# Operand distances, decays as products of gates, and a late root mean square in a two-block transformer kernel

## The chip, the cores and the metric

The kernel runs on one core of a Trainium2 chip. The metric is the device time of one launch in microseconds; the times below are runs of the same program with the same inputs.

## The reference

256 tokens of width 1024 pass through two kinds of blocks in float32. The first block has two layers of a hybrid mixer and an MLP with squared ReLU; the second has one layer of neighbourhood, dilated and memory attention and a mixture of 32 experts. The change touches the first block's mixers most.

```python
h = rms_norm(x, norm_mix[l])
(sq, sk, sv, dq, dk, dv, iq, ik, iw, hq, hf, hi, hg,
 g_sb, g_dsa, g_hg) = jnp.split(h @ w_in_l, ...)
# hgrn2, per head, chunk by chunk:
f = lb + (1.0 - lb) * sigmoid(hf);  k = 1.0 - f;  q = silu(hq)
b = cumsum(log f);  decay[t, s] = exp(b[t] - b[s]) for s <= t
att = einsum('tk,sk,tsk->ts', q, k, decay);  o = att @ hi + (q * exp(b)) @ S
# mixed = sigmoid(g_sb) * y_sb + sigmoid(g_dsa) * y_dsa + sigmoid(g_hg) * y_hg
x = x + mixed @ w_out_l
x = x + square(relu(rms_norm(x, norm_mlp[l]) @ w_up[l])) @ w_down[l]
```

y_sb comes from stick-breaking attention, y_dsa from a sparse attention that picks its 64 best keys by an index score, y_hg from the recurrence above.

## The kernel before

Each projection is done in three products of float32r parts (`mm3`: high times high, low times high, high times low). A weight tile comes in by a DMA on SP's queue into a ring of four tiles (`load`), ScalarE copies its high part and VectorE subtracts the low one (`split`). `proj_rows` takes tokens as the stationary and weights as the moving operand and gives rows of tokens; `proj_cols` takes weight blocks of 128 columns as the stationary and all 256 tokens as the moving operand and gives columns. The transposed parts of x, `xh` and `xl`, are made by a norm: `norm` squares x on ScalarE, takes the power on POOL, scales the rows on VectorE, transposes them on TensorE and splits them; `late_norm` transposes the unscaled x and leaves the factor to a later place (the MLP takes its square into the last addition). The two mixers use `norm`, the MLPs and the second block `late_norm`.

A mixer's projections are a list of chunks. `stream` prepares the next chunk (load and split) before the present chunk's products. At each yield of a chunk `step` moves the tasks that run beside it: the sparse attention (`dsa`, 1.5 steps a turn), the recurrence (`hgrn`, 3.5 steps, HG_RATE) and the stick-breaking attention (`sb`, 1.5). The order is that of the index and key projections, the recurrence's three, the gate of the recurrence, the stick-breaking projections, the two other gates, then the branches' output products and `w_out`. `dsa` waits with its softmax part until the recurrence's output is there; at the last gate `sigmoids` steps the tasks until all three outputs are there.

The recurrence works on levels of 64, 32, ... 1 tokens. For each level a 0/1 matrix (`lev`) sums the logarithms of the gates between a token and the middle of its block: TensorE multiplies the transposed, split logarithms `gh`, `gl` with it (`decays`, L679 and L680), ScalarE takes the exponential into `z`, VectorE and POOL multiply its halves with keys and queries (`scale`, L693 and L695), TensorE makes the small products (L715), and `join` puts them together.

Tiles lie in SBUF in the order in which the pools are opened: from the left the constants, the small tiles, the ring, `xh` and `xl`, then the tiles of 4 KB (`p4`), of 2 KB and the first block's own; from the right the tiles of 8 KB (`p8`) and the high and low parts of the weights (`split`). The distances between operands follow from the sizes of what lies between.

The experts' weights (192 pieces of 1 MB) are loaded into tiles as the dense stage frees them, and the expert stage runs through them in order.

Of the kernel before, what the change touches and what calls it, by code (L numbers as in the profile page):

```python
# [42 lines left out]
HG_RATE, DS_RATE, SB_RATE, NA_RATE, MEM_RATE, DIL_RATE = 3.5, 1.5, 1.5, 1.25, 1.5, 1.5  # L43
WAIT_X = {"km": 4, "qa0": 4, "qa1": 4, "ka": 5, "qm": 5, "qd": 4, "kd": 4}
WAIT_I, WAIT_O = 4, 7
WAIT_G, WAIT_H, WAIT_P, WAIT_S, WAIT_U = 3, 2, 2, 0, 2
# [4 lines left out]
C_MIX, C_MLP, C_MIX2, C_FFN2, C_MEM, C_LB, C_ON, C_QK, N_COLS = 0, 16, 32, 40, 48, 56, 64, 66, 72  # L51

# [3 lines left out]
def _constants():  # L56
# [8 lines left out]
    mats, sels = [], []  # L65
    for h in LEVELS:
        m = np.zeros((128, 128))
        for p in range(128):
            r = p // (2 * h) * 2 * h + h - 1
            if p > r:  # L70
                m[r + 1:p + 1, p] = 1
            else:
                m[p + 1:r + 1, p] = 1
        mats.append(m)
        if h < 32:

            s, t = i[:, None] % 32, i[None, :32]
            sels.append((s // (2 * h) == t // (2 * h)) & (s % (2 * h) < h) & (t % (2 * h) >= h))
    c["lev"] = np.concatenate(mats + [i[:, None] > i[None, :]] + mats[4:] + [i[:, None] <= i[None, :]], axis=1)
# [16 lines left out]
LATE = ("lev", "sel", "suffix")  # L96
CONST_AT, CONSTS = _constants()
N_KEEP = CONST_AT["lev"][0]
# [4 lines left out]
class Core:  # L103


    def __init__(self, tc, ctx, a, ring=4):
        self.tc, self.nc, self.a, self.ctx = tc, tc.nc, a, ctx
        nc = self.nc
        self.const = ctx.enter_context(tc.tile_pool(name="const", bufs=1))
        self.tiny = ctx.enter_context(tc.tile_pool(name="tiny", bufs=6))  # L110
        self.ring = ctx.enter_context(tc.tile_pool(name="ring", bufs=ring))
# [8 lines left out]
        self.tasks, self.of_table, self.set = [], [], None  # L120

    def open_dense(self, low, high):

        pool = lambda ctx, name, bufs, **side: ctx.enter_context(
            self.tc.tile_pool(name=name, bufs=bufs, reuse_waits="tile", **side))
        self.p8 = pool(self.ctx, "p8", 3, side="right")
        self.split_p = pool(low, "split", 4, side="right")
        self.xt = pool(self.ctx, "xt", 1)
        self.p4 = pool(self.ctx, "p4", 8)
        self.p2 = pool(high, "p2", 10)  # L130
        self.new_pool = pool
# [16 lines left out]
    def load_consts(self):  # L148
        nc = self.nc
        x = self.a["x"].rearrange("(t p) d -> p t d", p=128)  # L150
        for t in range(2):
            nc.sync.dma_start(self.x[:, t], x[:, t])
        nc.sync.dma_start(self.cst[:, :128], self.a["consts"][:, :128])
        nc.sync.dma_start(self.cols, self.a["cols"])
# [50 lines left out]
    def split(self, v):  # L205

        nc, k, n = self.nc, v.shape[1], v.shape[2]
        hi = self.split_p.tile([128, 1024], F32R, tag="hi", name="hi")
        lo = self.split_p.tile([128, 1024], F32R, tag="lo", name="lo")
        hi = hi[:, :k * n].rearrange("p (k n) -> p k n", n=n)  # L210
        lo = lo[:, :k * n].rearrange("p (k n) -> p k n", n=n)
        nc.scalar.activation(hi, v, AF.Copy)  # L212
        nc.vector.tensor_sub(lo, v, hi)  # L213
        return hi, lo

    def split_rows(self, v):
# [4 lines left out]
        for k0, k1 in ((0, cut), (cut, k)):  # L221
            if k1 > k0:
                hi, lo = self.split(v[:, k0:k1])
# [28 lines left out]
    def proj_rows(self, src, n, xs, kt, done, by_tile=False):  # L252
# [7 lines left out]
        def chunk(k0, k1):  # L260
# [5 lines left out]
            for i, (t, r) in enumerate(runs):  # L266
                x = xs(t)
# [12 lines left out]
    def proj_cols(self, src, n, xs, kt, done, early=None):  # L280
# [11 lines left out]
        def chunk(i):  # L292
            blocks = min(per, nb - i)
            v = self.load(src[:, i * 128:(i + blocks) * 128], kt, blocks * 128)
            ws = [self.split(v[:, :, j * 128:(j + m) * 128]) for j in range(0, blocks, m)]
# [41 lines left out]
    def norm(self, gain):  # L337


        nc = self.nc  # L340
        parts, ready = [], set()

        def task(t):
            if not parts:
                parts.extend(self.x_parts())
            xh, xl = parts
            x = self.x[:, t]
            xn = self.t4("xn")
            ms, rs = self.small(1, "ms"), self.small(1, "rs")
            nc.scalar.activation(xn, x, AF.Square, scale=1.0 / 32, accum_out=ms)  # L350
            self.rstd(rs, ms)
            for c in (slice(0, 512), slice(512, 1024)):
                nc.vector.tensor_scalar(xn[:, c], x[:, c], rs, None, op0=ALU.mult)
            yield
            yield
            tok = slice(t * 128, t * 128 + 128)
            for k0 in range(0, 8, 4):
                ps = self.ps().rearrange("p (m t) -> p m t", m=4)
                for m in range(4):
                    nc.tensor.transpose(ps[:, m], xn[:, (k0 + m) * 128:(k0 + m + 1) * 128], self.c("ident"))  # L360
                for m in range(4):
                    k = k0 + m
                    g = self.cols[:, gain + k:gain + k + 1]
                    nc.scalar.activation(xh[k][:, tok], ps[:, m], AF.Identity, scale=g)
                    nc.vector.scalar_tensor_tensor(xl[k][:, tok], ps[:, m], g, xh[k][:, tok], op0=ALU.mult, op1=ALU.subtract)  # L365
            ready.add(t)

        def get(t=None, k=8):
            self.until(lambda: ready >= ({0, 1} if t is None else {t}))
            return parts  # L370

        def start(t):
            g = task(t)
            next(g)
            self.start(g)
# [1643 lines left out]
```

## Time and profile before

| | us |
|---|---|
| median of 3 runs | 1496.46 |
| lowest, highest | 1493.56, 1496.97 |
| the profiled execution | 1495.28 |
| its span on the core | 1493.1 |

The profiled execution's time holds its span and 2.2 us around it. TensorE's granted clock was 0.947 on the mean. In the rows below a matmul's duration overlaps that of the next; how fast a stream of them runs is seen from their starts.

### The profile page before, as it was taken

The numbers are of one execution on the slowest core, as the hardware profiler recorded it, in microseconds if no ns is written. First come the engines' busy times: TensorE is split into PE (matmuls) and PEld (weight loads), VectorE is DVE, ScalarE is ACT, GpSimd is POOL, SyncE is SP. The second block draws the span as 40 slices with busy tenths as digits, with TensorE's granted clock in tenths as the row PEclk, the third lists the DMA queues.
The fourth block names the chain that finished last, engine by engine and source line by source line (L and its number), as shares of the span: only waits on it lengthen the run. The fifth ranks groups of instructions, "written<-read, shape, count | busy, mean of one in ns | idle before, by whom it ended". The sixth has DMA issues, their size and how long they took to land. (4 is left out here: it accounts for less than half of the span.)

```text
span 1493.1 us, 34069 instructions
## 1 busy us (share of the span) xinstructions
PE 1346.4 (90%) x14719; PEld 1182.5 (79%) x14719; DVE 746.3 (50%) x1378; ACT 661.0 (44%) x1182; POOL 153.7 (10%) x203
## 2 busy tenths in 40 slices
PE   7999999999999999999999999998777767766675
PEld 7889999989879889999898888897665655555453
DVE  6885768555565966677565565764111111111012
ACT  6664765544445556665454465863111111111111
POOL 2310011000002210020010025440000000000000
PEclk9999999999999999999999999999999978779777
DMA  9534446655546434366656657589999999999996
GB/s 298 173 108 135 133 149 201 197 182 186 197 121 198 148 95 141 109 227 209 219 180 193 234 187 182 161 330 392 387 415 417 415 417 417 416 417 415 404 418 264
DMA packets 172633, 376.40 MB, mean 252 GB/s; under 512 B 8321, under 2 KB 121137, under 8 KB 152641
## 3 DMA queue, kind: packets, MB, share of 16 engines
q1 hardware_dynamic: 169312, 366.67, 68.4%
q0 software_dynamic: 2880, 6.48, 1.5%
q8 instruction: 116, 1.90, 0.5%
q10 hardware_dynamic: 288, 1.05, 0.2%
q14 instruction: 37, 0.30, 0.1%
HBM read 372.07 MB, written 2.10 MB: 251 GB/s over the span
## 5 line engine op out<-in xcount | busy, mean ns | idle before, releaser
L213 DVE TENSOR_TENSOR lo<-w,hi 128x1024 fp32r<-128x1024 f32 (+3 forms) x334 | 387.6, 1163 | 257.5 <-ACT hi L212 256.3
L212 ACT ACTIVATE hi<-w 128x1024 fp32r<-128x1024 f32 (+3 forms) x334 | 333.4, 1001 | 318.5 <-PE ps L231 162.1
L230 PE MATMUL ps<-xh,hi 128*128 128x256 f32 x1120 | 317.4, 283 | 0.0
L232 PE MATMUL ps<-xh,lo 128*128 128x256 f32 x1120 | 312.4, 279 | 0.0
L231 PE MATMUL ps<-xl,hi 128*128 128x256 f32 x1120 | 312.3, 279 | 0.0
L1828 PE MATMUL hp<-we,xs 128*32 128x128 f32 x4096 | 154.5, 301 | 68.7 <-DMA we<-experts 57.2
L230 PEld LDWEIGHTS ps<-xh,hi 128*128 128x128 f32 x1120 | 210.4, 188 | 5.6 <-issue 3.7
L231 PEld LDWEIGHTS ps<-xl,hi 128*128 128x128 f32 x1120 | 210.4, 188 | 0.8
L232 PEld LDWEIGHTS ps<-xh,lo 128*128 128x128 f32 x1120 | 210.5, 188 | 0.0
L1828 PEld LDWEIGHTS hp<-we,xs 128*32 128x32 f32 x4096 | 122.4, 120 | 99.9 <-DMA we<-experts 67.4
L230 PE MATMUL ps<-hi,xh 128*128 128x256 f32 (+3 forms) x368 | 122.4, 334 | 0.0
L231 PE MATMUL ps<-lo,xh 128*128 128x256 f32 (+3 forms) x368 | 119.1, 325 | 0.8 <-DVE lo L213 0.8
L232 PE MATMUL ps<-hi,xl 128*128 128x256 f32 (+3 forms) x368 | 118.7, 325 | 1.2 <-DVE xl L365 1.2
L496 ACT ACTIVATE g<-hp 128x128 f32<-128x128 f32 x32 | 8.9, 277 | 224.9 <-PE hp L1828 224.9
L1869 PE MATMUL yp<-we,gT 128*32 128x128 f32 x2048 | 91.1, 335 | 18.8 <-ACT gT L1839 12.5
L230 PE MATMUL acc<-hi,hh 128*128 128x512 f32 x256 | 101.3, 396 | 0.0
L232 PE MATMUL acc<-hi,hl 128*128 128x512 f32 x256 | 101.1, 395 | 0.0
L231 PE MATMUL acc<-lo,hh 128*128 128x512 f32 x256 | 101.0, 395 | 0.0
L1869 PEld LDWEIGHTS yp<-we,gT 128*32 128x32 f32 x2048 | 71.0, 135 | 33.3 <-ACT gT L1839 20.9
L1833 DVE TENSOR_TENSOR g<-g,hp 128x128 f32<-128x128 f32 x28 | 8.1, 288 | 153.4 <-ACT g L496 153.4
L230 PEld LDWEIGHTS ps<-hi,xh 128*128 128x128 f32 x368 | 69.9, 191 | 5.3 <-issue 1.5
L232 PEld LDWEIGHTS ps<-hi,xl 128*128 128x128 f32 x368 | 69.6, 190 | 4.5 <-DVE xl L365 1.6
(530 smaller groups left out, 2024.9 us busy)
## 6 DMA issues: line engine op xcount, KB each, us to landing
we<-experts SPq DMA_DIRECT2D x155, 1024.0 KB, 17.5
w<-w_in SPq DMA_DIRECT2D x53, 1024.0 KB, 5.3
we<-experts SPq DMA_DIRECT2D x72, 512.0 KB, 15.5
w<-w_up SPq DMA_DIRECT2D x32, 1024.0 KB, 5.5
w<-w_down SPq DMA_DIRECT2D x32, 1024.0 KB, 4.9
w<-w_out SPq DMA_DIRECT2D x12, 1024.0 KB, 5.9
w<-w_in SPq DMA_DIRECT2D x36, 256.0 KB, 4.0
w<-w_in SPq DMA_DIRECT2D x8, 584.0 KB, 4.4
```

The lines of the kernel that those rows point to most:

```text
L212: nc.scalar.activation(hi, v, AF.Copy)
L213: nc.vector.tensor_sub(lo, v, hi)
L230: mm(out, l[0], r[0], start=first, stop=False)
L231: mm(out, l[0], r[1], start=False, stop=False)
L232: mm(out, l[1], r[0], start=False, stop=last)
L496: ins = self.nc.scalar.activation(out, x, func, **more)
L1828: nc.tensor.matmul(hp[j * 32:j * 32 + 32, wi], xs[:, k0 + kk, es], v[kk][:, j * 128:j * 128 + 128], start=k0 + kk == 0, stop=k0 + kk == 7)
L1833: nc.vector.tensor_mul(g, g, hp[:, 1])
L1869: nc.tensor.matmul(yp[j * 32:j * 32 + 32], gT[:, kk * 32:kk * 32 + 32], v[kk][:, j * 128:j * 128 + 128], start=kk == 0, stop=kk == 3)
```

## The change

- `pad_l`, `pad_r`, `pad_o` and the order of the pools put `xh`, `xl`, the tiles of 4 and 8 KB, the split weights and the branch outputs at one residue modulo 512 bytes, and `split` places its parts `at` a chosen offset: 80 floats for column blocks, 48 for rows under 512 wide, and for wider rows 80 in the first block and 0 in the second.
- `norm` is gone. The mixers use `late_norm`; `factors` makes the row factor `rs` for each token tile, and `by_column` spreads it over the partitions as `row`, by a product of ones with a diagonal. The places that read the mixer's projections multiply by one or the other: on ScalarE as a scale, or on VectorE.
- The recurrence has no logarithms, level matrices and exponentials. `whole` holds products of gates over 2, 4, ... 64 tokens (on POOL), and `grow` multiplies keys and queries in place from level to level, from the smallest upwards, both token tiles at once. HG_RATE is 1.
- `sb_project` waits for `dq` instead of `decays`; its queries and keys, and the gates that are not yet switched, leave PSUM through VectorE instead of ScalarE.
- First loads: identity and columns on ScalarE's queue, `load_later` behind the first chunk, `lev` not loaded, `warm` makes two products of zeros and a table load; the router's weights come in one contiguous transfer. The first layer's MLP ends by column halves like the second's.

```diff
-HG_RATE, DS_RATE, ... = 3.5, 1.5, 1.5, 1.25, 1.5, 1.5
+HG_RATE, DS_RATE, ... = 1, 1.5, 1.5, 1.25, 1.5, 1.5
+PAD_L, PAD_R, PAD_O = 8, 80, 40
+AT_COLS, AT_ROWS, AT_WIDE, PAD_W = 80, 48, (80, 0), 128
...
-    def split(self, v):
+    def split(self, v, at):
-        hi = self.split_p.tile([128, 1024], F32R, tag="hi", name="hi")
+        hi = self.split_p.tile([128, 1024 + PAD_W], F32R, tag="hi", name="hi")
-        hi = hi[:, :k * n].rearrange("p (k n) -> p k n", n=n)
+        hi = hi[:, at:at + k * n].rearrange("p (k n) -> p k n", n=n)
...
-                x = xs(t)
+                x = xs(t, k=r[1])
...
+        def factors(pool):
+            get.rs = [factor(t, pool.tile([128, 1], F32, name=f"rs_m{t}")) for t in range(2)]
+            def by_column():
+                get.row = pool.tile([128, T], F32, name="rs_row")
+                diag = self.t2("diag")[:, :T].rearrange("p (t n) -> p t n", t=2)
+                for t in range(2):
+                    nc.vector.tensor_scalar(diag[:, t], self.c("ident"), get.rs[t], None, op0=ALU.mult)
+                yield
+                ps = self.ps()[:, :T]
+                nc.tensor.matmul(ps, self.c("ones"), diag.rearrange("p t n -> p (t n)"), start=True, stop=True)
+                nc.scalar.activation(get.row, ps, AF.Copy)
...
         def q_done(i, ps):
-            k.sigmoid(s, ps)
-            nc.vector.tensor_mul(tile("hq")[:, i:i + 2], ps, s)
+            nc.vector.tensor_mul(q, ps, row(2))
+            k.sigmoid(s, q)
+            nc.vector.tensor_mul(q, q, s)
...
+        nc.vector.tensor_mul(q, hq, hg)
+        for h in reversed(LEVELS[:-1]):
+            whole[h] = tot[:, at:at + 4 * n].rearrange("p (h n) -> p h n", h=4)
+            u = whole[h // 2].rearrange("p h (n u) -> p h n u", u=2)
+            k.tc.keep_in_program_order(nc.gpsimd.tensor_mul(whole[h], u[:, :, :, 0], u[:, :, :, 1]))
...
+        def grow(h, keys, queries):
+            for x, tok, half in ((hk, keys, 0), (q, queries, 1)):
+                x = x[:, :, tok].rearrange("p h (b u w) -> p h b u w", u=2, w=h)[:, :, :, half]
+                w = whole[h][:, :, tok.start // h:tok.stop // h].rearrange("p h (b u) -> p h b u", u=2)[:, :, :, 1 - half]
+                nc.vector.tensor_mul(x, x, w[:, :, :, None].to_broadcast(list(x.shape)))
...
+        for lev in reversed(range(8)):
+            now = [(t, lev, products(t, lev)) for t in range(2)]
+            if lev == 0:
+                grow(64, slice(0, 128), slice(128, 256))
+            elif lev < 7:
+                grow(LEVELS[lev], slice(0, T), slice(0, T))
+            for j in last:
+                join(*j)
+            last = now
+            yield
...
                 g = gates[b][:, i:i + 2]
+                nc.vector.tensor_mul(g, ps, xs.norm.row[:, None, :].to_broadcast([128, 2, T]))
                 if switched:
-                    k.sigmoid(gates[b][:, i:i + 2], ps)
+                    k.sigmoid(g, g)
-                    nc.scalar.activation(gates[b][:, i:i + 2], ps, AF.Copy)
```

## Rows read from the trace of the kernel before

**Rows 1.** The page: engine shares; DMA busy tenths in 40 slices of the span.
```profile
PE 1346.4 (90%) x14719; PEld 1182.5 (79%) x14719; DVE 746.3 (50%) x1378; ACT 661.0 (44%) x1182; POOL 153.7 (10%) x203
...
DMA  9534446655546434366656657589999999999996
```

**Rows 2.** Busy time by stage: stretch, length, engines, granted clock, DMA share, GB/s.
```profile
60.00:120.00 60.00, 59.31 (x825) 52.99 (x824) 51.63 (x133) 35.18 (x59) 5.87 (x8) 1.00 0.38 115
120.00:210.00 90.00, 90.00 (x756) 85.62 (x756) 54.65 (x102) 59.62 (x115) 1.92 (x2) 1.00 0.40 124
...
290.00:437.00 147.00, 147.00 (x917) 131.26 (x915) 79.66 (x79) 67.60 (x78) 0.26 (x2) 1.00 0.57 182
437.00:449.00 12.00, 8.85 (x47) 7.66 (x46) 8.95 (x22) 7.28 (x19) 2.44 (x3) 0.72 0.21 63
...
870.00:1012.00 142.00, 141.78 (x1014) 125.17 (x1012) 96.41 (x185) 103.31 (x209) 64.90 (x74) 1.00 0.73 218
...
1050.00:1493.00 443.00, 316.34 (x6415) 239.54 (x6415) 63.50 (x182) 54.98 (x167) 0.00 (x0) 0.84 0.99 402
```

**Rows 3.** Timeline of TensorE in five stretches: start, duration, line, names, shape.
```profile
88.81 0.50 PE L680 MATMUL ps<-lev,gl 128*128 128x512 f32 x1 [0.69 <-DVE gl L423]
89.15 0.39 PE L679 MATMUL ps<-lev,gh 128*128 128x512 f32 x1
...
90.31 0.40 PE L680 MATMUL ps<-lev,gl 128*128 128x512 f32 x1
...
271.56 0.28 PE L230 MATMUL ps<-xh,hi 128*128 128x256 f32 x1
...
273.37 0.28 PE L231 MATMUL ps<-xl,hi 128*128 128x256 f32 x1
...
299.50 0.28 PE L231 MATMUL ps<-xl,hi 128*128 128x256 f32 x1
...
301.86 0.28 PE L230 MATMUL ps<-xh,hi 128*128 128x256 f32 x1
...
430.15 0.39 PE L230 MATMUL acc<-hi,hh 128*128 128x512 f32 x1
...
436.92 0.40 PE L232 MATMUL acc<-hi,hl 128*128 128x512 f32 x1
...
878.79 0.39 PE L231 MATMUL ps<-lo,memh 128*128 128x512 f32 x1
...
880.15 0.39 PE L231 MATMUL ps<-lo,memh 128*128 128x512 f32 x1
```

**Rows 4.** Groups of TensorE by line and shape: count, busy us, mean ns.
```profile
L230 PE MATMUL ps<-xh,hi 128*128 128x256 f32 x1120 | 317.4, 283 | 0.0
...
L230 PE MATMUL acc<-hi,hh 128*128 128x512 f32 x256 | 101.3, 396 | 0.0
...
L679 PE MATMUL ps<-lev,gh 128*128 128x512 f32 x32 | 14.6, 455 | 0.0
```

**Rows 5.** Timeline of TensorE where the second layer starts.
```profile
438.20 1.06 PE L360 MATMUL ps<-cst,xn 128*128 128x128 f32 x8 [0.89 <-DVE xn L353]
```

**Rows 6.** Timeline of TensorE at the start.
```profile
10.91 0.46 PE L230 MATMUL ps<-hi,xh 128*128 128x256 f32 x1
12.14 0.39 PE L231 MATMUL ps<-lo,xh 128*128 128x256 f32 x1 [0.77 <-DVE lo L213]
```

**Rows 7.** Groups of VectorE by line and shape, 60 to 240 us.
```profile
L695 DVE TENSOR_TENSOR z<-z,hq 128x256 f32<-128x256 f32 x14 | 7.3, 535 | 1.0 <-ACT z L496 1.0
...
L779 DVE TENSOR_TENSOR o<-o,rs 128x512 f32<-128x512 f32 x1 | 0.7, 693 | 2.1 <-POOL rs L324 2.1
```

**Rows 8.** Timeline of POOL and VectorE from 219.5 us, and VectorE's group.
```profile
220.14 8.40 POOL L1072 TENSOR_TENSOR gate<-gate 128x512 f32<-128x512 f32 x4 [91.10 <-ACT hi L212]
...
220.06 0.96 DVE L213 TENSOR_TENSOR lo<-w,hi 128x768 fp32r<-128x768 f32 x1
...
L213 DVE TENSOR_TENSOR lo<-w,hi 128x768 fp32r<-128x768 f32 x12 | 11.5, 956 | 2.5 <-ACT hi L212 2.2
```

## Prediction before the result

> **What bounds the kernel now.** I read the engine shares of the page first, then the table by stage. TensorE is busy 90% of the span and the DMA line turns from 4 to 7 tenths into a solid 9 over the last third [rows 1]. The stages say why [rows 2]. From 60 to 437 us and from 870 to 1012 us TensorE's busy time equals the stage within 1.2%, with the DMA engines at 0.38 to 0.73. From 1050 us on TensorE has 316 of 443 us and the DMA engines 0.99: that stage waits for expert weights. So up to about 1012 us every microsecond taken out of TensorE's stream counts if VectorE keeps up. The expert loads need tiles that the dense stage frees, so when that stage ends earlier they start earlier, by the same amount.
>
> A busy time of matmuls overlaps, so I read starts instead. The same 128x256 product with the same operands starts every 113 ns in one stretch (271.56 to 273.37, 16 steps) and every 118 ns in another (299.50 to 301.86, 20 steps) [rows 3]. The 128x512 products of the MLP start every 233 ns (430.15 to 436.92, 29 steps), those of the memory projection every 227 ns (878.79 to 880.15, 6 steps) [rows 3]. So there are two levels, 4% and 3% apart, at the full clock.
>
> **The decays (gain).** The level matrices go: 32 pairs of 128x512 matmuls in the two layers [rows 4]. Inside a run they start every 0.232 us (89.15 to 90.31, 5 steps) [rows 3], so 64 cost at least 14.8 us. One that follows a wait or a small product lasts 0.1 us longer, 0.50 for 0.39 [rows 3]; the first ones' mean of 455 ns [rows 4] adds 2 us for 32. With a wait of 0.69 us for an operand in each layer [rows 3] and the 16 transposes of the log gates (about 0.11 us, an estimate from the 118 ns of the larger products) I take 20 us. ScalarE's exponentials and logarithm go too; ScalarE has slack (35 of 60 us) [rows 2].
>
> **The norm at the start of the second layer (gain).** Between 437 and 449 us TensorE issued 47 instructions at a granted clock of 0.72, that is partly at 1.2 GHz [rows 2], because the transposes waited for the scaled rows [rows 5]. 16 transposes at 0.11 and 31 products at 0.118 would need 5.4 of these 12 us. The edit transposes the unscaled rows of the first half while the second half's products still run, and the first chunk asks for k below 4 first: 12 products for each of two token tiles, 2.8 us, cover the last additions, transposes and copies. I take 5.5 of the 6.6 us. The square and the power then hide behind that chunk; without that cover they would cost about 2.5 us.
>
> **The start (gain).** The first product starts at 10.91 us, right after the first weights' copy, and the next waits 0.77 us for the low half of the weights [rows 6], while VectorE and ScalarE still make the parts of x. With x transposed as it lands, its parts are ready before the weights are, so the first product stays near 10.9 but the stutter behind it goes: 2 us, between 0 and 3. Moving two small loads from SP's queue to ScalarE's puts the first weight load about 0.9 us forward, behind 1 MB of x all the same; 0.8 MB of level matrices is no longer fetched there. The two products of zeros run while TensorE is idle: nothing. The loads moved to POOL behind the first chunk, the contiguous router load and the new pool for small tiles: nothing, all are used 10 us or more later.
>
> **The distances (gain, uncertain).** Adding up the tiles in the order in which the pools are opened, stationary minus moving address is now, modulo 512 bytes, 192 for column blocks and 320 for rows and for the MLP's second product. After, it is 320 for both kinds of 256-wide product, 192 for the 512-wide rows of the first block and 0 for those of the second. What before shows: 256 wide at 192, both levels, mostly the high one; 256 wide at 320, both; 512 wide at 320, always the high one; 512 wide at 0, the low one. 512 wide at 192 it doesn't show. If all 3,360 products of column blocks (three lines of 1,120) went from 118 to 113.2 ns and all 768 of the MLP (three of 256) from 233.4 to 226.7 [rows 3, 4], that is 16 + 5 = 21 us. Part already runs low, and both levels occur at one distance, so what ran before a product matters too. I take half, 11 us; below nothing, because a stretch that is low now may turn high, at most about a third of the first sum, -5 us.
>
> The Trainium skill, page "TensorE: Matmul & The Clock Gate", section "Step-by-step: what each phase is for", says that the moving operand and the weight load have read ports of their own, so that loading weights takes nothing from the running matmul. By that rule the distances do nothing and this term is 0, the first rival below. The 512-wide pair of spacings agrees badly with it, the 256-wide pair neither way.
>
> **What is added.** Two ones-products of 128x256 with their copy: 1 us on TensorE in all. On VectorE, in the stretch that had 51.63 busy of 60 us [rows 2]: removed are 24 half-level products (14 at 0.535 us, the others near it), two low halves and two end products at 0.69, together 15 us a layer. Added are 15 products of 128x512 with a broadcast operand (0.693 by the nearest row), 10.4 us, and in that stretch eight products with the factor's row at the same price, 5.5 us [rows 7]. So VectorE has 52.5 us in a stretch that TensorE would now do in 50: 2.5 to 3 us a layer, 6 in all. The strided halves may cost as the strided products do now, 0.535 for 256 elements, so 1.07: then 8.5 us a layer, 17 in all; and 0 if the next stretch takes the backlog. I take 6, since one broadcast row of the same size is the nearer one. POOL's six gate products, 2.1 us and less [rows 8], run beside it.
>
> The Trainium skill, page "SBUF — State Buffer", section "Who interferes with whom", says that VectorE with two operands in SBUF and GpSimd reading SBUF shut each other out for a whole instruction. By it the gate products would hold VectorE up to 4.5 us more a layer, which makes the sum 1475. The trace disagrees on VectorE's side: a low half of 128x768 took 0.96 us beside a POOL product and 0.956 on the mean [rows 8], so the sum leaves it out.
>
> **The slower recurrence.** The task now moves one step a turn instead of 3.5. Counting turns: its output comes at turn 45 instead of 35, the sparse attention that waits for it ends at turn 60 instead of 50, and the last gate block is through at 58. The last two turns then run with no projection beside them: 1 us a layer if later branch products fill in, 3 us if not. I take 2 in all.
>
> **Sum.** -20 - 5.5 - 2 - 11 + 1 + 6 + 2 = -29.5. The profiled execution took 1495.28 us, 1.2 below the median of 1496.46: 1495.3 - 29.5 = 1465.8, so 1466.
>
> **Rivals.**
> - The distances do nothing: 1466 + 11 = 1477. For: both levels at one distance. Against: 512-wide at 0 and at 320.
> - VectorE binds in the recurrence: 17 instead of 6, 1477; with the first rival too, 1488. For: 51.63 of 60. Against: 54.65 of 90 us in the stretch behind it [rows 2], which can take a backlog.
> - All goes right: distances 21, no backlog, no idle turns: 1466 - 10 - 6 - 2 = 1448.
> - VectorE stands still beside POOL's gate products. One of 128x512 takes 2.1 us [rows 8], the halves behind it as much again at most: 4.5 us a layer, 9 in all, 1475. Against: 0.96 beside 0.956 [rows 8].
> - Slower: a serial chain. Each level's products read what the two multiplications behind the last level wrote, in place. If TensorE's order puts them at the head, it waits for two at 1.07 and for one weight split of 1.22 ahead of them: 3.36 us for 7 levels in 2 layers, 47 us. That would stand in place of the 6: 1466 + 41 = 1507. It decides from 2.5 us a level on (35 us in all). Against: one turn brings 24 products, 2.7 us of cover.
> - No change: the expert loads set the end whatever the dense stage does: 1495. For: 0.99 from 1050. Against: 0.73 before 1012.
>
> **Chances.** Forecast (1456 to 1472) 0.36, no effect of the distances 0.25, VectorE with or without it 0.12, all right 0.16, POOL 0.02, chain 0.05, no change 0.04. The range that leaves out 2 in 10 is 1444 to 1484. About 0.3%, 4.5 us, is what a measurement of this kernel can tell from no change. Faster 0.90, same 0.05, slower 0.05.
>
> **What would show it.** No level products; no stretch below the full clock near 430 us, and no wait above 0.5 us there; the column blocks at 113 ns and the MLP's second product at 227 ns; VectorE near 10 tenths in the recurrence, but TensorE without waits for it; the dense stage ending near 982 us and the last stage as long as before. It is wrong if the spacings rise to 120 ns, if TensorE waits for VectorE at each level, or if the expert stage grows by what the dense stage lost.

## The result and the profile after

The changed kernel takes 1476.73 us (median of 4 runs, 1474.38 to 1478.39), the one before 1496.2 in the same comparison: a ratio of 0.9872, 95% interval 0.9854 to 0.989. That is 1.3% faster, inside the predicted range of 1444 to 1484, but outside the forecast's own 1456 to 1472 and 10.7 us above the predicted 1466; it lies at the times of three of the rivals (1475 and 1477), so the time alone does not tell which account is right. The profiled execution took 1474.38 us with a span of 1472.6.

The page after the change, as in [rows 1]: engine shares, and the DMA engines' busy tenths in 40 slices.

```profile
PE 1322.0 (90%) x14647; PEld 1164.7 (79%) x14647; DVE 754.3 (51%) x1369; ACT 628.5 (43%) x1099; POOL 148.7 (10%) x205
...
DMA  8645336655547445266656658599999999999997
```

The stages of the changed kernel, answering to [rows 2]: stretch, length, busy time and instructions of each engine, granted clock, DMA share, GB/s.

```profile
60.00:120.00 60.00, 57.28 (x860) 54.31 (x859) 58.48 (x139) 26.27 (x40) 7.24 (x13) 1.00 0.43 133
120.00:210.00 90.00, 88.88 (x745) 83.43 (x745) 60.23 (x110) 53.94 (x103) 1.92 (x2) 1.00 0.42 130
...
430.00:442.00 12.00, 11.10 (x96) 10.81 (x95) 9.01 (x18) 10.15 (x22) 1.58 (x4) 1.00 0.22 56
853.00:994.00 141.00, 140.82 (x1012) 124.79 (x1010) 94.28 (x184) 102.88 (x209) 65.46 (x74) 1.00 0.73 219
1030.00:1472.00 442.00, 315.82 (x6479) 238.28 (x6467) 63.55 (x182) 55.25 (x168) 0.00 (x0) 0.85 0.99 404
```

TensorE is still the bound of the dense stages and the expert stage is as long as before. Three things differ. At 430 us, where the second layer starts, the clock stays at 1.00 and 96 instructions go through in 12 us, for 47 at 0.72 before. From 60 to 120 us VectorE has 58.48 of 60 us, for 51.63, and TensorE stands idle for 2.7 us, for 0.7. And from 120 to 210 us TensorE, which had no hole there, has 1.1 us of them.

For the account I read, in three traces, when TensorE starts a product that every version has. The third trace is the run with the old distances (first experiment): it has every edit but the distances of the weights' tiles. The indexer parts are the transposes for the index score; branch 2 is the recurrence's output product, the first of the three branches.

```
start, us                            before    after   old distances
first product of the indexer parts    45.81    47.54    47.33
first product of branch 2, layer 1   211.33   205.29   206.41
first down product of MLP 1          279.72   276.46   280.02
last down product of MLP 1           436.92   429.56   437.23
indexer parts, layer 2               477.89   465.28   473.27
branch 2, layer 2                    643.50   623.73   632.25
first down product of MLP 2          711.88   696.54   705.73
last down product of MLP 2           870.44   852.88   864.27
last output product of the dense part 1028.29 1010.37  1022.42
last product of the experts         1488.75  1468.15  1481.98
```

Differences between neighbouring lines of the first and the last column give the terms without the distances. Start: +1.5. From the indexer to branch 2, where the decays are grown: -6.4 and -6.6 in the two layers. From branch 2 to the MLP's down products: +5.2 and +5.1. From MLP 1 to the second layer's indexer: -4.9. The rest of the dense part: within 0.3 of 0. Expert stage: -0.9.

### The profile page after: what moved, and what is told of

Read it like the earlier page. It is cut to its first block, busy times and chain, and to the rows that moved or that the text cites. A ratio compares the mean times of both kernels' runs of the same rounds, so it can differ in the third digit from the quotient of the medians.

```text
span 1472.6 us, 33788 instructions
## 1 busy us (share of the span) xinstructions
PE 1322.0 (90%) x14647; PEld 1164.7 (79%) x14647; DVE 754.3 (51%) x1369; ACT 628.5 (43%) x1099; POOL 148.7 (10%) x205
## 5 line engine op out<-in xcount | busy, mean ns | idle before, releaser
L242 PE MATMUL ps<-xh,hi 128*128 128x256 f32 x1120 | 318.2, 284 | 0.0
L242 PEld LDWEIGHTS ps<-xh,hi 128*128 128x128 f32 x1120 | 211.2, 189 | 7.2 <-issue 4.7
L242 PE MATMUL ps<-hi,xh 128*128 128x256 f32 (+3 forms) x368 | 122.0, 333 | 4.1 <-ACT hi L220 3.2
L242 PE MATMUL acc<-hi,hh 128*128 128x512 f32 x256 | 99.9, 390 | 0.0
L1840 PEld LDWEIGHTS yp<-we,gT 128*32 128x32 f32 x2048 | 66.4, 128 | 41.3 <-ACT gT L1810 21.3
L242 PEld LDWEIGHTS ps<-hi,xh 128*128 128x128 f32 x368 | 70.3, 191 | 8.1 <-ACT hi L220 3.5
L243 PEld LDWEIGHTS ps<-lo,xh 128*128 128x128 f32 x368 | 70.5, 191 | 3.3 <-DVE lo L221 0.8
```

Of the source, the lines that this page charges most:

```text
L242: mm(out, l[0], r[0], start=first, stop=False)
L243: mm(out, l[0], r[1], start=False, stop=False)
L1840: nc.tensor.matmul(yp[j * 32:j * 32 + 32], gT[:, kk * 32:kk * 32 + 32], v[kk][:, j * 128:j * 128 + 128], start=kk == 0, stop=kk == 3)
```

## The experiments

The ratios are to the kernel before, run on the same chip in the same rounds; the changed kernel stands at 0.9872.

**1. Old distances.** Only addresses change; each engine issues the same instructions in the same order.

```diff
-AT_COLS, AT_ROWS, AT_WIDE, PAD_W = 80, 48, (80, 0), 128
+AT_COLS, AT_ROWS, AT_WIDE, PAD_W = 48, 48, (48, 48), 128
```

> The changed kernel with the distances of before: all offsets of the split tiles 48 elements, so that column blocks stand at 192 and rows and the 512-wide products at 320 bytes modulo 512; every engine issues the same instructions in the same order. If the distances set the spacing, the product spacings go back to 117 ns (256 wide, mean) and 233 ns (512 wide), TensorE's stream grows by about 12 us, and the kernel takes 1476.7 + 12 = 1489 us. If the distances do nothing, 1477 us within 2 us, and the spacings stay at 115 and 228 ns.

Measured: 1487.07 us, ratio 0.9947 (0.9933 to 0.9961). The distances are worth 0.0075 of 1496, 11.2 us, give or take 3 by the two intervals; the dense part of the two traces differs by 12.0 us. Two kinds of product do not stand as before the change here: the branch products at 192 instead of 320, and the memory projection and the last output product, 512 wide, at 320 instead of 0. At 6 ns each for 144 products, by the spacings below, the latter is about 1 us.

**2. All distances 0.**

```diff
+AT_COLS, AT_ROWS, AT_WIDE, PAD_W = 0, 0, (0, 0), 128
```

> The changed kernel with all offsets of the split tiles 0, so that stationary and moving operand stand at 0 bytes modulo 512 everywhere (before, only the 512-wide products of the memory projection stood there, at 227 to 229 ns). If the distances set the spacing and 0 is the best of them for every width, the 256-wide products fall from 115 to 113.3 ns and the 384-wide ones from 175 to 170: 1476.7 - 9 = 1468 us. If 0 is good for 512 alone, or what ran before a product decides, between 1475 and 1485. If the distances do nothing, 1477 us within 2 us.

Measured: 1487.66 us, 0.995 (0.9937 to 0.9964). 0 is good for 512 alone; the time is above the 1475 to 1485 that I had given for that.

**3. Distance 384 for the column blocks and the rows below 512, 0 for the 512-wide.**

```diff
+AT_COLS, AT_ROWS, AT_WIDE, PAD_W = 96, 32, (0, 0), 128
```

> The changed kernel with both kinds of 256-wide product, and the 384- and 292-wide ones, at a distance of 384 bytes modulo 512, and all 512-wide ones at 0. Measured so far for 256 wide: 119.8 ns at 0, 117.3 at 192, 114.8 at 320. If the spacing keeps falling with the distance, 113.5 ns at 384, 5 us less: 1472. If it is periodic and rises again towards 512, which is 0, 116 to 118 ns, 5 to 13 us more: 1482 to 1489. The 512-wide ones start every 227.5 ns in either case.

Measured: 1486.48 us, 0.995 (0.9936 to 0.9964). The spacing rises again behind 320.

The same 22 products of the first MLP's column blocks in four kernels. TensorE's timeline; L242 starts every third product, so the two lines of each kernel stand 21 products apart. First the changed kernel, at 320:

```profile
265.58 0.28 PE L242 MATMUL ps<-xh,hi 128*128 128x256 f32 x1
...
267.96 0.28 PE L242 MATMUL ps<-xh,hi 128*128 128x256 f32 x1
```

The old distance, 192:

```profile
268.72 0.28 PE L242 MATMUL ps<-xh,hi 128*128 128x256 f32 x1
...
271.19 0.28 PE L242 MATMUL ps<-xh,hi 128*128 128x256 f32 x1
```

Distance 384:

```profile
267.37 0.28 PE L242 MATMUL ps<-xh,hi 128*128 128x256 f32 x1
...
269.86 0.28 PE L242 MATMUL ps<-xh,hi 128*128 128x256 f32 x1
```

Distance 0:

```profile
270.05 0.28 PE L242 MATMUL ps<-xh,hi 128*128 128x256 f32 x1
...
272.57 0.28 PE L242 MATMUL ps<-xh,hi 128*128 128x256 f32 x1
```

Divided by 21: 113, 118, 119 and 120 ns. The duration reads 0.28 in each line; only the starts tell them apart. At 0 and at 384 all column blocks of the MLPs run at 119 to 120 ns. At 192 and at 320 the two levels of the prediction occur both. In the kernel before, at 192, the same 22 products start every 113 ns, and those behind its first 512-wide products every 118 [rows 3]. In the changed kernel, at 320, the column blocks of the second MLP start every 113 ns up to its first 512-wide products (677.84 to 680.22 us, 21 steps) and every 118 behind them, where the kernel before has the same pattern. The first two lines are of the kernel before, the other two of the changed one, 21 steps each:

```profile
268.84 0.28 PE L230 MATMUL ps<-xh,hi 128*128 128x256 f32 x1
...
271.22 0.28 PE L230 MATMUL ps<-xh,hi 128*128 128x256 f32 x1
...
707.45 0.28 PE L242 MATMUL ps<-xh,hi 128*128 128x256 f32 x1
...
709.92 0.28 PE L242 MATMUL ps<-xh,hi 128*128 128x256 f32 x1
```

The 512-wide products of the MLP, 12 apart: the changed kernel in layer 1 (at 192) and in layer 2 (at 0).

```profile
281.95 0.39 PE L242 MATMUL acc<-hi,hh 128*128 128x512 f32 x1
...
284.70 0.39 PE L242 MATMUL acc<-hi,hh 128*128 128x512 f32 x1
...
702.01 0.39 PE L242 MATMUL acc<-hi,hh 128*128 128x512 f32 x1
...
704.73 0.39 PE L242 MATMUL acc<-hi,hh 128*128 128x512 f32 x1
```

And the old distance, 320, 9 apart:

```profile
285.63 0.39 PE L242 MATMUL acc<-hi,hh 128*128 128x512 f32 x1
...
287.73 0.39 PE L242 MATMUL acc<-hi,hh 128*128 128x512 f32 x1
```

229, 227 and 233 ns. Only addresses differ between the changed kernel and those of experiments 1 to 3, so the address changes the spacing, and of the distances tried the best for one width is the worst for the other: 320 for 256 wide, 0 for 512 wide. It is not the place of the weights by itself: adding up the tiles, the 512-wide weights stand at 480 modulo 512 in the kernel before (233 ns) and in the first MLP of the changed one (229 ns), and at 352 in the run with the old distances (233 ns); the distance fits all three. What ran before counts too, as the second MLP shows. In the first MLP, whose 512-wide products stand at 192, the column blocks keep 113 ns to the end; whether their own 320 or that 192 does it, no run separates. In the mixers, with few 512-wide products among them, the column blocks run mostly at 113 ns in the changed kernel and mostly at 118 with the old distances.

**4 and 5. The start.** Two more products of zeros behind the transposes of x; or none at all.

```diff
         norms[0]()
+        ps = core.ps()
+        for _ in range(2):
+            core.tc.keep_in_program_order(core.nc.tensor.matmul(ps, core.zeros[:, :128], core.zeros, start=True, stop=True))
```

> The changed kernel with two more products of zeros (128x512, four passes of 0.85 us) pinned behind the 16 transposes of x at the start, where TensorE stands idle from 8.1 to 11.3 us. If that idle time, behind some work, is why the granted clock is 0.50 from 10.9 to 17.8 us, the clock stays at 1.0 there, the products of this stretch start every 0.113 instead of 0.213 us, some 30 of them, and the dense stage ends 3 us earlier: 1474 us. The rival: those products wait for the next weights anyway, or the fill itself delays them, and the time stays at 1477 within 1 us.

> The changed kernel without its two products of zeros at the start. If the idle time from 8.1 to 11.3 us behind any work lowers the clock, the transposes alone do it too: granted clock 0.50 from about 11 to 18 us as now, 1477 us. The rival: the zeros started what lowered it (TensorE's first work then comes at 4.9 instead of 1.4 us); then the clock stays at 1.0 over the first products, as before the change, and the time falls by 3 us to 1474.

Measured: 1475.07 us, 0.987 (0.9854 to 0.9885), and 1475.51 us, 0.9871 (0.9856 to 0.9886): neither can be told from the changed kernel by its time. Inside the profile the fill lets the 96th product, the last of the first chunk, start at 25.34 instead of 26.32 us. It ends at 9.6 us, because its own four passes take 1.9 us in all where the first four took 3.8, so it covers half of the hole. Without the zeros the first products start every 0.21 us up to 16.7 us all the same (rows in the last section): the slow start does not need them, and the rival is out. The last experiment has a longer fill; the rows stand there.

**6. The rate of 3.5 again.**

```diff
-HG_RATE, DS_RATE, SB_RATE, NA_RATE, MEM_RATE, DIL_RATE = 1, 1.5, 1.5, 1.25, 1.5, 1.5
+HG_RATE, DS_RATE, SB_RATE, NA_RATE, MEM_RATE, DIL_RATE = 3.5, 1.5, 1.5, 1.25, 1.5, 1.5
```

> The changed kernel with the recurrence's rate back at 3.5 steps a turn. My theory: at one step a turn 24 products (2.7 us) cover the two multiplications behind each level; at 3.5 three levels come in one turn without cover, so TensorE waits for VectorE at most of the 7 levels of each layer, 1.3 to 2.5 us each: 10 to 25 us lost, less 8 us that come back because the sparse attention ends earlier and the gates' sigmoids no longer stand before the weight casts (waits near 211 and 630 us gone): 1479 to 1495 us. The rival: VectorE was ahead anyway, no wait at the levels, and only the gain at the end is seen: 1469 us.

**7. A rate of 2**, in the same place.

> The changed kernel with 2 steps a turn instead of 1. My theory: the recurrence's output comes about 6 turns earlier, the table switch and the three gates' sigmoids (6.8 us of ScalarE) come before the last gate block is through, so the waits of 2.1 us for a weight cast near 211 and 630 us go with the 0.7 us ones around them, -6 to -8 us; but only 12 products (1.4 us) cover the two multiplications of a level, so TensorE waits about 0.5 to 1.5 us more at half of the levels, +4 to +10: between 1473 and 1481. The rival: the wait near 211 us has another cause (the slot of the tile, the DMA of the weights), then it stays, and the kernel takes 1481 to 1487.

Measured: 3.5 gives 1481.25 us, 0.9897 (0.988 to 0.9913); 2 gives 1474.28, 0.9853 (0.9836 to 0.9869). In both, the waits before the weight casts near 211 and 630 us are gone, and TensorE waits at the levels instead: at 3.5 it waits 10.4 us for the grown factors and 4.6 us for the queries. The chain of the slower rival exists; one step a turn is what hides it.

**8. Twice the growing.** Each multiplication is followed by one that leaves the values as they are.

```diff
                 nc.vector.tensor_mul(x, x, w[:, :, :, None].to_broadcast(list(x.shape)))
+                nc.vector.tensor_tensor(x, x, x, op=ALU.max)
```

> The changed kernel with a second VectorE instruction of the same size behind each of the multiplications that grow the decays (the larger of the product and itself, which leaves the values as they are): about 0.6 us more on VectorE for 26 instructions, 16 to 18 us in all, in the chain between the levels. If VectorE sets the pace in the recurrence, the kernel takes all of it: 1493. If it has slack, the extra work disappears except where TensorE waits already (one level a layer): 1477 to 1481. My theory is in between, nearer to slack: the chain of a level grows from 1.3 to 2.5 us, which with one weight split in the queue exceeds the 2.7 us of cover at some levels: 1482.

Measured: 1486.52 us, 0.9933 (0.9916 to 0.995), by the ratios 9.1 us more. Added were 24 instructions of 0.69 us and 4 of 0.42, 18.2 us, and TensorE's waits for them rose from 5.0 to 14.1 us. So VectorE had room for about half of it: less slack than I had thought.

**9. All transposes of the second layer behind the last addition.**

```diff
-                        if t:
-                            then.start(2 * c)
-                            then.start(2 * c + 1)
+                        if t and (l or c):
+                            for q in range(2 * c if l else 0, 2 * c + 2):
+                                then.start(q)
```

> The changed kernel with all four groups of transposes at the start of the second layer issued behind the last addition of the MLP, instead of two of them while the second half's products still run. If those two groups are what covers the last additions, transposes and copies, TensorE waits 1 to 2.5 us longer near 430 us (0.94 us now) and perhaps falls below the full clock there: 1479 us. The rival: the second half's additions and copies set that wait alone, and the first half's groups pass in the same time: 1477 us within 1 us.

Measured: 1476.22 us, 0.9867 (0.9849 to 0.9885). The rival is right: those two groups cover nothing that counts. What is left is the unscaled rows and the order of the first chunk, which no run tells apart.

**10. Two turns before the transposes of the recurrence's output.**

```diff
-WAIT_I, WAIT_O = 4, 7
+WAIT_I, WAIT_O = 4, 2
```

> The changed kernel with the recurrence still at one step a turn, but with 2 instead of 7 turns between its normalised output and the transposes of it, so that the sparse attention that waits for this output begins 5 turns earlier. My theory: the 10 us by which the end of each mixer grew (waits of 0.7, 1.0 and 2.4 us near 191, 204 and 211 us, the same in the second layer, and the half clock behind them) come from that output alone; they go, nothing else changes in the recurrence, and the kernel takes 1476.7 - 9 = 1468 us. The rival: ScalarE's table switch and the three sigmoids (6.8 us) stand before a weight cast wherever they come; then the wait of 2 us only moves to an earlier place and the kernel takes 1474 to 1477.

Measured: 1465.79 us, 0.9806 (0.9793 to 0.982), the fastest of all, by the ratios 9.9 us below the changed kernel. First the changed kernel at the end of the mixer, ScalarE and then TensorE:

```profile
205.70 1.28 ACT L471 ACT_TABLE_LOAD   x1
207.00 5.52 ACT L482 ACTIVATE gate<-gate 128x2048 f32<-128x2048 f32 x3
212.42 3.03 ACT L220 ACTIVATE hi<-w 128x768 fp32r<-128x768 f32 x4
...
213.29 0.39 PE L242 MATMUL ps<-ds_hi,hi 128*128 128x256 f32 x1 [2.08 <-ACT hi L220]
```

The same work of ScalarE with two turns:

```profile
195.56 1.28 ACT L471 ACT_TABLE_LOAD   x1
196.85 1.91 ACT L482 ACTIVATE gate<-gate 128x2048 f32<-128x2048 f32 x1
...
198.93 3.28 ACT L482 ACTIVATE gate<-gate 128x2048 f32<-128x2048 f32 x2
```

The table load and the three sigmoids take 6.8 us in the one and 6.6 in the other. In the changed kernel they come when gate 0 is through and the next weights' casts are due, and TensorE stands; 10 us earlier they run beside gate 0's products and TensorE waits for nothing between 195 and 240 us. From branch 2 to the MLP's down products it takes 68.5 us in both layers of this run, as it did before the change.

**11. The recurrence begun 4 turns later, the output at the same turn.**

```diff
-WAIT_I, WAIT_O = 4, 7
+WAIT_I, WAIT_O = 4, 3
@@ hgrn
+        for _ in range(4):
+            yield
         both = self.t8("qd_tot")
```

> The changed kernel with the recurrence begun 4 turns later, and those 4 turns taken from the 7 between its output and the transposes, so that the output comes at the same turn as now. By then the search for the largest scores of the sparse attention has left VectorE's queue. My theory: the wait of 2.2 us of TensorE at the second level (94 and 512 us; the two multiplications stood behind eight instructions of that search) goes, with the 0.8 us behind it and the half clock that follows in one layer: 1476.7 - 6 to 8 = 1470 us. The late waits near 211 and 630 us stay. The rival: VectorE is simply full in this stretch; then the wait turns up at other levels, or the weight splits come late, and the kernel takes 1475 to 1478.

Measured: 1471.81 us, 0.9845 (0.983 to 0.986), by the ratios 4 us below the changed kernel. VectorE's queue and TensorE in the changed kernel around the second level:

```profile
91.49 0.61 DVE L868 MAX8 m<-score 128x8 f32<-128x128 f32 x2
...
93.06 0.68 DVE L669 TENSOR_TENSOR hk<-hk,hg 128x512 f32<-128x512 f32 x1
93.66 0.68 DVE L669 TENSOR_TENSOR qd_tot<-qd_tot,hg 128x512 f32<-128x512 f32 x1
...
88.59 0.76 PE L686 MATMUL ps<-qd_tot,hk 128*32 128x32 f32 x64
94.48 0.96 PE L686 MATMUL ps<-qd_tot,hk 128*32 128x32 f32 x64 [2.20 <-DVE qd_tot L669]
```

The operands of this level were free at 89.3 us, when the level before had been read. A weight split and the search for the largest scores (MAX8, MATCH) came first, and the growing began at 93.06. With the search out of the way TensorE waits 1.6 us in its place, behind weight splits, so the rival has a share: VectorE is nearly full here. The intervals of the two ratios overlap a little, so the 4 us are only just clear of noise.

**12. Together**, with a longer fill at the start.

```diff
-WAIT_I, WAIT_O = 4, 7
+WAIT_I, WAIT_O = 2, 1
@@ hgrn
+        for _ in range(1):
+            yield
         both = self.t8("qd_tot")
@@ chunks, behind norms[0]()
+        for _ in range(4):   # products of zeros, as in the fourth experiment
```

> The changed kernel with what the runs so far point to: the recurrence begun 1 turn later and 1 turn instead of 7 between its output and the transposes (so the output comes 5 turns earlier, as in the run with 2 turns there), the sparse attention's first transposes after 2 steps instead of 4, so that its search for the largest scores leaves VectorE's queue before the first level's two multiplications, and four products of zeros behind the first transposes, where TensorE stands idle from 8.1 to 11.3 us. My theory: the gains add up, 9.8 us for the end of the mixers, 3 to 5 for the second level, 1 to 2 for the start: 1476.7 - 15 = 1461 us. The rival: the one turn that is left before the transposes doesn't cover the output's normalisation on VectorE, or the search only collides with other work; then 1464 to 1468, no better than with the 2 turns alone.

Measured: 1468.32 us, 0.9819 (0.9806 to 0.9833): no better than the two turns alone. The level waits fell to 0.65 us and less, and the start came right, but the indexer's transposes, two steps earlier, now wait for POOL's rotation, 1.35 us in layer 1 and 2.54 in layer 2, there with a stretch at a granted clock of 0.50 about it (457.8 to 461.2 us):

```profile
41.25 0.55 PE L436 MATMUL ps<-cst,iqk 128*128 128x128 f32 x3 [1.35 <-POOL iqk L771]
...
458.46 0.90 PE L436 MATMUL ps<-cst,iqk 128*128 128x128 f32 x3 [2.54 <-POOL iqk L771]
```

The start in the changed kernel, where [rows 6] stood before; TensorE's timeline, then two stretches as in the table of stages (TensorE's busy time and count come first, the granted clock is the third number from the end):

```profile
4.93 3.18 PE L364 MATMUL ps<-cst,x 128*128 128x128 f32 x16
11.33 0.80 PE L242 MATMUL ps<-hi,xh 128*128 128x256 f32 x2 [3.22 <-ACT hi L220]
...
11.00:14.00 3.00, 2.20 (x8) 1.91 (x9) 2.68 (x4) 3.00 (x5) 0.57 (x2) 0.50 1.08 358
14.00:18.00 4.00, 4.00 (x22) 4.00 (x21) 2.36 (x2) 2.50 (x5) 3.83 (x8) 0.53 0.85 216
```

With the hole filled up to 11.4 us:

```profile
11.00:14.00 3.00, 2.25 (x15) 1.62 (x14) 2.75 (x4) 3.00 (x5) 0.48 (x2) 1.00 1.08 357
14.00:18.00 4.00, 4.00 (x37) 4.00 (x37) 2.63 (x3) 3.75 (x7) 3.83 (x8) 1.00 0.88 228
```

The first product is no earlier (11.41), but 37 products go through in the 4 us from 14 that had 22, and the 96th product starts at 23.87 instead of 26.32 us. So the hole of 3.2 us in front of the first weights cost 2.4 us more behind it, at a granted clock near 0.50, that is 1.2 GHz.

## Why the prediction was right in sign and 10.7 us off

**The distances** were taken as -11 of a possible 21: measured -11.2. The half was a hedge and no mechanism, so an agreement this close is luck. By the mean of back-to-back starts in the two traces, the 512-wide products (232.7 to 228.3 ns) gave all of their 5 us and the 256-wide ones (116.6 to 114.9) about 7 of their 16: the column blocks came to 113 ns, as forecast, in the first MLP and most of the mixers, and stayed mostly at 118 in the second MLP. The rival that the distances do nothing is out, though the time itself fell on its 1477. So is, for this kernel, what the prediction drew from the rule of the Trainium skill, "TensorE: Matmul & The Clock Gate", "Step-by-step: what each phase is for", that the two read ports keep weight loads and the moving operand apart: the same products in the same order start every 113 to 120 ns when only addresses change.

**The decays, with VectorE and the ones-products** (-20 + 6 + 1 = -13): measured -13.1. The level products are gone. That the sum agrees to 0.1 us is luck in part: from start to start, the level products, their transposes and the wait took 10.8 and 11.1 us in the two layers before, 21.9 in all for the 20; and in the run with the old distances, from which the 13.1 comes, TensorE waits 3.6 us at the levels and 1.8 for the sparse attention's values, which belong to the slower recurrence. The 6 us were near in size and wrong in shape: I had an even backlog, and the trace of the changed kernel has one level in each layer behind the search (5.0 us of waits in all, at three places) and one stretch of half clock behind such a wait; the rival of 17 us is out. The price of 0.693 us for a growing multiplication was right (0.68). The serial chain, 47 us, did not come: 24 products a turn cover it, as argued, and at 3.5 steps a turn they don't.

**POOL beside VectorE** was left out of the sum on [rows 8], and that was too quick. POOL's gate products run from 69.9 to 74.2 us, and a weight split beside them takes 1.78 us, where it takes 1.21 at 63.68 us:

```profile
63.68 1.21 DVE L221 TENSOR_TENSOR lo<-w,hi 128x1024 fp32r<-128x1024 f32 x1
...
70.45 1.78 DVE L221 TENSOR_TENSOR lo<-w,hi 128x1024 fp32r<-128x1024 f32 x1 [0.20 <-ACT hi L220]
...
71.23 3.00 POOL L656 TENSOR_TENSOR qd_tot<-qd_tot 128x256 f32<-128x256 f32 x5
```

The three short instructions behind it take 1.60 us, for 1.10 at 64.81 us: together 1.1 us of VectorE a layer, for the 4.5 of the rival. The Trainium skill, "SBUF — State Buffer", "Who interferes with whom", that the two engines shut each other out, is right here, against what I wrote: the gate product that runs when the split starts (69.94 us, 1.21 long) ends 0.7 us later, and the split lost 0.57. The row that I had against it could not show it: its split starts at 220.06, ahead of the POOL product at 220.14 [rows 8]. At that time TensorE waits for nothing, so it cost no time that I can show.

**The norm** (-5.5): measured -4.9. A wait as long as the one that [rows 5] had at 438.20 is still there with 0.90 us, but the two that the kernel before had behind it are gone and the clock stays up (1.00 from 430 to 442 us). The kernel before, then the changed one:

```profile
440.56 0.38 PE L232 MATMUL ps<-hi,xl 128*128 128x256 f32 x1 [0.77 <-DVE xl L365]
443.04 1.51 PE L360 MATMUL ps<-cst,xn 128*128 128x128 f32 x6 [1.46 <-DVE xn L353]
...
431.73 0.39 PE L242 MATMUL ps<-hi,xh 128*128 128x256 f32 x1 [0.90 <-ACT xh L369]
```

One of the two reasons that I gave, transposes under the second half's products, is worth nothing (experiment 9). And "no wait above 0.5 us there" was wrong.

**The start** (-2, between 0 and 3): measured +1.5, outside these bounds. I had put the zeros down as nothing because TensorE is idle then, and the early transposes as a pure gain. They moved its first work ahead and left 3.2 us of idle time just before the first weights, where before the transposes ran into the first product without a hole; the products behind it ran at half clock to 17.8 us. Nor were the 2 us to be had: with the hole filled (experiment 12) the 96th product starts at 23.87 us, 0.6 before the 24.43 of the kernel before.

**The slower recurrence** (+2) is the step that failed: measured +10.3. I had counted the turns rightly, the sparse attention ending after the last gate block, and costed the last turns as turns without a projection, 1 to 3 us a layer. What I had not asked is what ScalarE has to do once that attention ends: the table load and the sigmoids of all three gates, 6.8 us, ahead of the casts of the next weights. From branch 2 to the down products of the run with the old distances I find 2.3 us a layer of waits for the casts and, in both layers, a stretch of half clock behind them, about 1.6 us by the estimate in the last section; 1.3 us of the 5.2 stay without a row. With two turns the whole of it goes (68.5 us, experiment 10). One constant outside the diff, the 7 turns between the output and its transposes, took two turns' time at 3.5 steps a turn and seven at 1; setting it to 2 gave 9.9 us back, give or take 3.

**The sum** with what was measured: -13.1 - 4.9 + 1.5 + 10.3 - 11.2 - 0.9 = -18.3, for 19.1 by the ratio (0.0128 of 1496). The miss of 10.7 us is 8.3 at the end of the mixers, 3.5 at the start and 0.6 at the norm, less 1.7 in what remains. The expert stage kept its length, so the dense part's gain came through, as forecast.

## What to carry to other kernels

Where a change alters the pace of one task, look up each waiting count that is given in that task's own steps, and ask what every engine does when the task ends, ScalarE's table switch above all. Read the spacing of matmul starts, not their durations, and try the offset between stationary and moving tile for each width by itself, since here the best one differed and 0.7% of the kernel hung on it; then try them together, since one width's choice went with the other's spacing. Idle time of TensorE just before a dense stretch was paid almost twice here (3.2 us and 2.4 behind it); if early work leaves such a hole, fill it to its end.

## What the runs showed of the hardware that I had not expected

A wait of TensorE of some 2 us, in a stream that is full before and behind it, was often followed by a stretch at half the granted clock, and not always. In the changed kernel one follows the wait of 2.26 us that ends at 512.29 us, none the wait of 2.20 that ends at 94.48 nor the one of 2.08 that ends at 213.29; in the run with the old distances one follows each of the waits of 2.08 us that end at 214.41 and 640.26. The wait of 0.90 us that ends at 431.73 had no such stretch. The wait at 512, two products of 128x256 behind it that stand 10 steps apart, the stretch and the one behind it:

```profile
512.29 0.90 PE L686 MATMUL ps<-qd_tot,hk 128*32 128x32 f32 x64 [2.26 <-DVE qd_tot L669]
...
513.72 0.41 PE L244 MATMUL ps<-xh,lo 128*128 128x256 f32 x1
...
515.85 0.40 PE L242 MATMUL ps<-xh,hi 128*128 128x256 f32 x1
...
512.70:516.10 3.40, 3.40 (x53) 3.34 (x41) 3.40 (x9) 0.00 (x0) 0.00 (x0) 0.50 0.03 8
516.10:520.00 3.90, 3.90 (x92) 3.73 (x92) 3.90 (x11) 1.06 (x1) 0.00 (x0) 1.00 0.28 57
```

The counts mix widths; the products of 128x256 start every 0.213 us in the stretch and every 0.113 at the full clock. By an estimate from these, the 3.4 us from 512.70 cost about 1.6 us on top of the wait.

The granted clock of a row is not always the speed of the products. Without the zeros (experiment 5) the row from 14 to 18 us reads 1.00 with 25 products, where the filled start of experiment 12 had 37, and just before it they start every 0.21 us (two steps in the lines), about twice the 0.113 us of the full clock:

```profile
14.00:18.00 4.00, 4.00 (x25) 4.00 (x25) 2.36 (x2) 2.84 (x5) 3.83 (x8) 1.00 0.86 225
...
13.31 0.41 PE L237 MATMUL ps<-hi,xh 128*128 128x256 f32 x1
...
13.74 0.41 PE L239 MATMUL ps<-hi,xl 128*128 128x256 f32 x1
```

Why the products fall into levels by address, and why both levels occur at one distance, stays open. So does which of the two distances, the column blocks' own or that of the 512-wide products among them, keeps the first MLP at the lower level. A distance of 192 for the 512-wide products of the second layer, which might give its column blocks the lower level back, was not tried.
